# A decoder step on one core: ScalarE's DMAs issued by GpSimd, and the first head's loads of the prompt attention ahead of other work

## The chip, the core and the metric

The kernel runs on one core of a Trainium2 chip. A core has five engines with a queue of instructions each, worked in order: TensorE (PE), VectorE (DVE), ScalarE (ACT), GpSimd (POOL) and SyncE (SP, which here only issues DMAs). SP, ACT and POOL can issue DMAs; an instruction that waits for a semaphore holds all that stand behind it on its engine. PE's clock has two levels here, 1.2 and 2.4 GHz; the profile gives the granted clock as a part of full speed. The metric is the time of one execution on the device in microseconds (us), lower is better.

## The reference

One layer of a decoder, for a prompt of 1024 rows and 8 samples of 8 new tokens with a window of 2048 cached keys and values, all in float32:

```python
yp = _half_ffn(yp, ffn1_norm[l], ffn1_w1[l], ffn1_w3[l], ffn1_w2[l])
m, kp, vp, sp = _mix_prompt(_rmsnorm(yp, mix_norm[l]), ...)
yp = yp + m
yp = _half_ffn(yp, ffn2_norm[l], ffn2_w1[l], ffn2_w3[l], ffn2_w2[l])
# the same for the samples, ys, with _mix_sample over the cached window and the state
```

`_half_ffn` is x + (silu(h w1) * (h w3)) w2 / 2 on the normalised h. The mixing step projects h to queries, keys and values of 12 heads of 64 (queries and keys normalised by head) and to queries, keys, values, gates and decays of 4 heads of a gated linear attention (GLA). The 12 heads attend in three dilated branches, whose results are merged by their log-sums; the GLA runs in chunks of 16 with a state between chunks. Both go, the GLA normalised and gated with silu(rb), through `w_out`. Returned are both outputs, the windows of keys and values (for the samples: the cached rows moved on by the 8 new ones) and the GLA states.

## The kernel before

The kernel's stages follow each other on PE, in us from the span's start: the first FFN to about 822, a mixed stage to 1244, the prompt attention to 1519, the output projection to about 1612, the second FFN to 2400. A float32 operand is split into a high and a low part, and a product is made of three matmuls.

In the mixed stage `_interleave` (L1271) runs two programs side by side. `inputs` makes the projections column block by column block: for each, weights are loaded by SP (`raw`), split (`hl`), multiplied into PSUM (`psg`, L306) in three pieces of rows, and a piece is turned and stored. `beside` is first the GLA within its chunks, then the attention of the samples (`sample`), which for each of six pairs of heads loads keys `kt` (3 buffers), values `vt` (6 buffers) and biases `sbias` by SP.

The stores that ACT issues before are these. For a block of values, `turn_values` (L421) transposes a piece on PE into `psv` (L427, L429), ACT copies it to `v` (L431, L433; 4 buffers) and stores it to the output `vp` (L439), the samples' rows also to `vnew` (L434) and to the output `wv_s` (L435). `finish_gate` (L443) stores the gates to `gsc` (L446). `sample` stores new keys (`sko` to `wk`, L817) and its outputs (`soT` to `osc`, two stores, L907). POOL's queue holds, in `finish_qk` (L451), the stores of queries to `qsc` and of keys to `kT` (L473) and the copies of the samples' part (`sqk`, L475), and in `sample` the copies from it to `sqs` (L810) and `kt` (L827); `psA` (L831) is the score product of the samples with `kt`.

In the prompt attention a second `_interleave` (L1280) runs `attention` and `linear_states` side by side. `attention` loads a head's `f` (queries from `qsc`, keys from `kT`, each in two halves of 64 rows, L929) and `bias` (L937), for every second head `va` (L940); DVE makes `q` and `kk` of them (L932 to L935; for later heads POOL makes the low parts); PE makes scores `psS` (L962), DVE adds the bias and takes the maximum (`e`, L969), ACT the exponentials (L982), PE transposes (L1001) and multiplies with `va` (`psO`, L1022). `linear_states` loads `g7` from `gsc` and `asc` (L596, L598), makes `gw` and `qm` of it on DVE (L611 to L621), and clears `st` and `qm` on POOL (L585, L590).

A scheduler sets the order on each engine: it plays the program on a model of the engines, and `high_priority` moves what is written under it ahead by an offset. It also hands out the semaphores by which a DMA tells its end. DMAs of SP and of ACT take eight of them in turn (DMAHW0 to DMAHW7), those of POOL eight others (DMASW0 to DMASW7); a DMA waits until the one before it on its semaphore has landed.

Of the kernel before, what the change touches and what calls it, by code (L numbers as in the profile page):

```python
# [9 lines left out]
F32 = mybir.dt.float32  # L10
# [6 lines left out]
P = 128  # L17
# [103 lines left out]
class _Kernel:  # L121
# [299 lines left out]
    def turn_values(self, pool, ps, z, m, ci):  # L421
        nc, a = self.nc, self.a
        cols = slice(128 * m, 128 * m + 128)
        t0, nt = 3 * ci, 3 if ci < 2 else 2
        p = ps.tile([P, 512], F32, tag="b", name="psv")
# [6 lines left out]
        if ci == 2:  # L432
            nc.scalar.copy(v[:64, 2], p[:64, 256:384])  # L433
            nc.scalar.dma_start(out=self.vnew[:, cols], in_=v[:64, 2])  # L434
            nc.scalar.dma_start(  # L435
                out=a["wv_s"].rearrange("b (r c) -> b r c", c=768)[:, 2040:2048, cols], in_=v[:64, 2]
            )
            self.vdone = m + 1
        nc.scalar.dma_start(  # L439
            out=a["vp"][128 * t0 : 128 * (t0 + nt), cols].rearrange("(t p) c -> p t c", p=P), in_=v[:, :nt]  # L440
        )

    def finish_gate(self, z, m, ci):  # L443
        nc = self.nc
        nc.scalar.activation(z, z, AF.Silu)
        nc.scalar.dma_start(  # L446
            out=self.gsc[3 * ci : 3 * ci + 3, :, 5 + m].rearrange("t p r -> p t r"),
            in_=z.rearrange("p (t r) -> p t r", t=3),
        )
# [131 lines left out]
    def linear_states(self, pool, ps):  # L581

        nc, a = self.nc, self.a
        st = pool.tile([P, 9, 64], F32, tag="st", name="st", bufs=2)
        nc.gpsimd.memset(st[:, 0], 0.0)  # L585
        ms = pool.tile([P, 3, 36], F32, tag="gms", name="gms")
        qm = []
# [48 lines left out]
        for T in range(9):  # L636
# [11 lines left out]
            for j, src in enumerate((kdT, g[:, 3], g[:, 4])):  # L648
# [3 lines left out]
                out=kx,  # L652
# [125 lines left out]
    def sample(self, pool, ps, loadk):  # L778
# [18 lines left out]
        for i in range(6):  # L797
# [8 lines left out]
            for e in range(2):  # L806
# [9 lines left out]
            nc.scalar.copy(ko, p[:64, :128])  # L816
            nc.scalar.dma_start(  # L817
                out=a["wk"].rearrange("b (r c) -> b r c", c=768)[:, 2040:2048, 128 * i : 128 * i + 128], in_=ko
# [87 lines left out]
            for e in range(2):  # L906
                nc.scalar.dma_start(  # L907
                    out=self.osc[i, 64 * e : 64 * e + 64].rearrange("p (b t) -> p b t", t=8), in_=t[:, :, e]
                )
# [3 lines left out]

    def attention(self, inputs, pool, ps):
        nc = self.nc
        heads = {}

        def load(h):
# [18 lines left out]
            nc.sync.dma_start(out=b, in_=bass.AP(z.tensor, z.offset + 127, [[GW - 1, P], [1, NP]]))  # L937
            if e == 0:
                v = pool.tile([P, 8, 128], F32, tag="v", name="va", bufs=2)
                nc.sync.dma_start(  # L940
                    out=v, in_=self.a["vp"][:, 128 * i : 128 * i + 128].rearrange("(t p) c -> p t c", p=P)
                )
            else:
                v = heads[h - 1][3]
            heads[h] = (q, kh, kl, v, b)

        def scores(h, g):

            q, kh, kl, v, b = heads[h]
            out = []  # L950
# [58 lines left out]
        def weigh(h, g, es, pts):  # L1009
            i, e = h // 2, h % 2  # L1010
            r = slice(64 * e, 64 * e + 64)
            v = heads[h][3]
            if g % 2 == 0 and e == 0:
# [26 lines left out]
        self.tc.keep_in_program_order(nc.scalar.preload_act_table_set(LOG_EXP))  # L1040
        load(0)
        yield 10
# [104 lines left out]
    def run(self):  # L1147
        nc, tc, a = self.nc, self.tc, self.a
        self.gready, self.done, self.vdone = False, 0, 0
        with ExitStack() as top:  # L1150
            self.dram = top.enter_context(tc.tile_pool(name="dram", bufs=1, space=DRAM))
# [121 lines left out]
            with ExitStack() as hs:  # L1273
                hpool(hs)
                with ExitStack() as bs:
# [3 lines left out]
                    states = (4.6 * c for c in self.linear_states(gp, ps0))  # L1279
                    _interleave(tc, [(self.attention(ip, ap, ps0), 0), (states, 0)])  # L1280
                with pool("wts") as wp, pool("xp", side="right") as xp:
# [165 lines left out]
```

## Time and profile before

| | us |
|---|---|
| three executions | 2400.91, 2401.41, 2404.52 (median 2401.41) |
| the profiled execution, its time | 2401.93 |
| its span, first to last instruction | 2400.1 |
| its mean granted clock of PE | 0.989 |
| PE busy | 2341.4 |
| DVE, ACT, POOL busy | 1155.9, 656.9, 408.3 |

The profile is of one execution. PE is the engine that is busy nearly throughout, so the reader should look for the stretches where it isn't, and then for what ended last before it went on. ACT's DMA queue moves 5.11 MB in 16512 packets, SP's 316.39 MB.

### The profile page before, as it was taken

What the parts mean: (1) busy time and instruction counts of PE and PEld (TensorE: products, weight loads), DVE (VectorE), ACT (ScalarE), POOL (GpSimd) and SP (SyncE); (2) the same over time, 40 slices, a digit from 0 to 9 for tenths busy, and PEclk for the clock granted to TensorE, in tenths of its full rate; (3) what the DMA queues carried; (4) which work ended last, traced back from release to release, by engine and by line L of the source; (5) the groups of instructions that cost most, each with busy time, mean ns of one, the idle gap of its engine ahead of it and who ended that gap; (6) DMA issues with size and microseconds to landing.
All of it is one profiled execution on the core that took longest, in us unless ns stands there. A gap on an engine that the chain in (4) does not pass through costs nothing.

```text
span 2400.1 us, 38321 instructions
## 1 busy us (share of the span) xinstructions
PE 2341.4 (98%) x16073; PEld 2215.0 (92%) x16073; DVE 1155.9 (48%) x2377; ACT 656.9 (27%) x1347; POOL 408.3 (17%) x303
## 2 busy tenths in 40 slices
PE   7999999999999998999989999999999999999999
PEld 6999999999999987978767767999999999999999
DVE  8452434344342753555538887435444342434333
ACT  5111020101101522545436666334111101020110
POOL 5011020101100400011103231333101101020100
PEclk9999999999999999999999999999999999999999
DMA  7346542524250334599865442414244243111002
GB/s 258 110 162 192 191 152 97 210 97 153 86 196 23 134 131 108 179 342 341 310 184 130 111 115 74 156 36 158 88 163 153 92 154 143 45 53 45 28 17 85
DMA packets 135261, 330.25 MB, mean 138 GB/s; under 512 B 25920, under 2 KB 105264, under 8 KB 127408
## 3 DMA queue, kind: packets, MB, share of 16 engines
q1 hardware_dynamic: 116464, 316.39, 38.7%
q10 hardware_dynamic: 16512, 5.11, 0.9%
q0 software_dynamic: 2112, 6.29, 0.7%
q8 instruction: 126, 2.06, 0.3%
q14 instruction: 47, 0.39, 0.0%
HBM read 300.55 MB, written 134.56 MB: 181 GB/s over the span
## 4 chain that ended last, share of the span: by engine, by line
PE 89%; DVE 5%; DMA 3%; ACT 2%; issue 1%; SPq 1%; POOL 0%; ACTq 0%; DVEq 0%; POOLq 0%
PE ps L306 42%; PE ps L257 21%; PE psg L306 12%; PE pso L306 4%; PE psO L1022 2%; PE psS L962 2%; PE psW L880 1%; PE psT L1001 1%; DMA vt<-in_vin 1%; PE psA L831 1%; DVE hL L155 1%; DVE e L969 1%; PE pss L459 1%; DMA f<-out_kT 0%; DVE rstd L170 0%
## 5 line engine op out<-in xcount | busy, mean ns | idle before, releaser
L306 PE MATMUL ps<-hH,hl 128*128 128x362 f32 (+1 forms) x4224 | 1044.1, 328 | 8.1 <-ACT hl L130 6.8
L306 PEld LDWEIGHTS ps<-hH,hl 128*128 128x128 f32 x4224 | 746.6, 188 | 12.4 <-ACT hl L130 6.7
L306 PE MATMUL ps<-hL,hl 128*128 128x362 f32 (+1 forms) x2112 | 691.5, 328 | 2.9 <-DVE hL L155 2.9
L257 PE MATMUL ps<-g,hl 128*128 128x362 f32 (+1 forms) x3168 | 529.2, 328 | 0.0
L257 PEld LDWEIGHTS ps<-g,hl 128*128 128x128 f32 x3168 | 527.0, 188 | 0.0
L134 POOL TENSOR_TENSOR hl<-raw,hl 128x1024 fp32r<-128x1024 f32 (+1 forms) x98 | 242.8, 2498 | 1223.3 <-ACT hl L130 1223.3
L306 PEld LDWEIGHTS ps<-hL,hl 128*128 128x128 f32 x2112 | 397.5, 188 | 4.9 <-DVE hL L155 3.9
L306 PE MATMUL psg<-hH,hl 128*128 128x384 f32 (+3 forms) x1200 | 312.4, 334 | 0.0
L262 DVE SCALAR_TENSOR_TENSOR xT<-ps,xT 128x362 f32<-128x362 f32 (+1 forms) x384 | 204.6, 534 | 200.3 <-PE ps L257 191.4
L217 ACT ACTIVATE t<-t 128x364 f32<-128x364 f32 x132 | 66.9, 508 | 786.0 <-DVE t L216 785.8
L218 DVE TENSOR_TENSOR t<-ps,rstd 128x364 f32<-128x364 f32 x132 | 70.6, 535 | 417.9 <-PE ps L306 417.9
L306 PEld LDWEIGHTS psg<-hH,hl 128*128 128x128 f32 (+1 forms) x1200 | 211.3, 186 | 12.8 <-issue 8.9
L306 PE MATMUL psg<-hL,hl 128*128 128x384 f32 (+3 forms) x600 | 200.1, 334 | 0.1
L130 ACT CAST hl<-raw 128x1024 fp32r<-128x1024 f32 (+2 forms) x148 | 124.1, 886 | 187.3 <-PE ps L306 109.9
L130 ACT CAST g<-t 128x364 fp32r<-128x364 f32 x132 | 65.2, 494 | 346.8 <-DVE t L219 346.8
L134 DVE TENSOR_TENSOR g<-t,g 128x364 fp32r<-128x364 f32 x132 | 107.1, 813 | 92.8 <-ACT g L130 92.5
L216 DVE TENSOR_TENSOR t<-ps,rstd 128x364 f32<-128x364 f32 x132 | 70.5, 535 | 156.6 <-PE ps L306 155.3
L306 PEld LDWEIGHTS psg<-hL,hl 128*128 128x128 f32 (+1 forms) x600 | 111.7, 186 | 9.3 <-issue 6.7
L134 DVE TENSOR_TENSOR hl<-raw,hl 128x384 fp32r<-128x384 f32 (+3 forms) x178 | 102.9, 587 | 23.9 <-ACT hl L130 19.9
L962 PE MATMUL psS<-kk,q 128*128 128x512 f32 (+2 forms) x288 | 92.2, 411 | 19.6 <-DVE s L969 11.9
L306 PE MATMUL pso<-hH,hl 128*128 128x362 f32 (+1 forms) x384 | 93.6, 325 | 0.2 <-DVE o L1032 0.2
L982 ACT ACTIVATE e<-e,s 128x128 f32<-128x128 f32 (+3 forms) x96 | 74.9, 780 | 43.7 <-DVE s L969 43.1
(205 smaller groups left out, 2007.2 us busy)
## 6 DMA issues: line engine op xcount, KB each, us to landing
out_wk<-in_ck SPq DMA_DIRECT2D x16, 3060.0 KB
out_wv_s<-in_cv SPq DMA_DIRECT2D x16, 3060.0 KB
kt<-in_kin SPq DMA_DIRECT2D x24, 1280.0 KB
vt<-in_vin SPq DMA_DIRECT2D x60, 512.0 KB
raw<-in_w13b SPq DMA_DIRECT2D x22, 1024.0 KB
raw<-in_w13a SPq DMA_DIRECT2D x21, 1024.0 KB
raw<-in_w2a SPq DMA_DIRECT2D x48, 192.0 KB
raw<-in_w2b SPq DMA_DIRECT2D x48, 192.0 KB
```

The lines of the kernel that those rows point to most:

```text
L130: nc.scalar.copy(hi, x)
L134: e.tensor_tensor(out=lo, in0=x, in1=hi.bitcast(F32), op=ALU.subtract)
L155: nc.vector.scalar_tensor_tensor(out=self.hL[:, k, s], in0=x, scalar=g, in1=self.hH[:, k, s].bitcast(F32), op0=ALU.mult, op1=ALU.subtract)
L216: nc.vector.tensor_tensor(out=t1[:, :n], in0=p1[:, :n], in1=r, op=ALU.mult)
L217: nc.scalar.activation(t1[:, :n], t1[:, :n], AF.Silu)
L218: nc.vector.tensor_tensor(out=t3[:, :n], in0=p3[:, :n], in1=r, op=ALU.mult)
L257: self.mm(p[:, :n], lhsT=hl[:, wt, j, :], rhs=g[:, gp, :n], start=i == 0, stop=i == 3 * nf - 1)
L262: nc.vector.scalar_tensor_tensor(out=xs, in0=p[:, :n], scalar=0.5, in1=xs, op0=ALU.mult, op1=ALU.add)
L306: self.mm(p[:m, :n], lhsT=hl[:, wt, k, cs], rhs=h[:, k, h0 : h0 + n], start=i == 0, stop=i == 23)
L962: self.mm(p[:, :mm], lhsT=q[:, 128 * n : 128 * n + 128], rhs=kk[:, o : o + mm], start=x == 0, stop=x == 1,)
L982: nc.scalar.activation(e[:, :w], e[:, :w], AF.Exp, scale=-1.0, bias=s[:, j : j + 1], accum_out=s[:, 2:3])
L1022: self.mm(p[64 * n : 64 * n + 64, :128], lhsT=v[:, k, r], rhs=pts[k // 2][k, n], start=k == 0, stop=k == 2 * g + n, tile_position=(0, 64 * n),
```

## The change

All DMAs that ACT issued are issued by POOL. The load of `va` becomes a method, `load_v`: the first is written at the start of `linear_states`, the others stay in `attention`'s `load` for even heads; its buffers move from the pool `att` to `gst`. `load(0)` stands under `high_priority(offset=300)`. The two programs of the prompt attention are handed to `_interleave` in the other order. A head's raw rows come in two transfers for each operand, as before. Lines after L586 have numbers one to eight higher in the changed kernel.

```diff
@@ turn_values @@
         nc.scalar.copy(v[:, :nt].rearrange("p t c -> p (t c)"), p[:, : 128 * nt])
         if ci == 2:
             nc.scalar.copy(v[:64, 2], p[:64, 256:384])
-            nc.scalar.dma_start(out=self.vnew[:, cols], in_=v[:64, 2])
-            nc.scalar.dma_start(
+            nc.gpsimd.dma_start(out=self.vnew[:, cols], in_=v[:64, 2])
+            nc.gpsimd.dma_start(
                 out=a["wv_s"].rearrange("b (r c) -> b r c", c=768)[:, 2040:2048, cols], in_=v[:64, 2]
             )
             self.vdone = m + 1
-        nc.scalar.dma_start(
+        nc.gpsimd.dma_start(
             out=a["vp"][128 * t0 : 128 * (t0 + nt), cols].rearrange("(t p) c -> p t c", p=P), in_=v[:, :nt]
         )
@@ finish_gate @@
         nc.scalar.activation(z, z, AF.Silu)
-        nc.scalar.dma_start(
+        nc.gpsimd.dma_start(
             out=self.gsc[3 * ci : 3 * ci + 3, :, 5 + m].rearrange("t p r -> p t r"),
@@ linear_states @@
         nc.gpsimd.memset(st[:, 0], 0.0)
+        self.load_v(pool, 0)
@@ sample @@
             nc.scalar.copy(ko, p[:64, :128])
-            nc.scalar.dma_start(
+            nc.gpsimd.dma_start(
                 out=a["wk"].rearrange("b (r c) -> b r c", c=768)[:, 2040:2048, 128 * i : 128 * i + 128], in_=ko
             )
...
             for e in range(2):
-                nc.scalar.dma_start(
+                nc.gpsimd.dma_start(
                     out=self.osc[i, 64 * e : 64 * e + 64].rearrange("p (b t) -> p b t", t=8), in_=t[:, :, e]
                 )
@@ new, and attention @@
+    def load_v(self, pool, i):
+        v = pool.tile([P, 8, 128], F32, tag="v", name="va", bufs=2)
+        self.nc.sync.dma_start(
+            out=v, in_=self.a["vp"][:, 128 * i : 128 * i + 128].rearrange("(t p) c -> p t c", p=P)
+        )
+        self.values[i] = v
+
-    def attention(self, inputs, pool, ps):
+    def attention(self, inputs, pool, vpool, ps):
...
-            if e == 0:
-                v = pool.tile([P, 8, 128], F32, tag="v", name="va", bufs=2)
-                nc.sync.dma_start(
-                    out=v, in_=self.a["vp"][:, 128 * i : 128 * i + 128].rearrange("(t p) c -> p t c", p=P)
-                )
-            else:
-                v = heads[h - 1][3]
-            heads[h] = (q, kh, kl, v, b)
+            if h % 2 == 0 and h:
+                load_v(i)
+            heads[h] = (q, kh, kl, b)
...
-        load(0)
+        with self.tc.high_priority(offset=300):
+            load(0)
@@ run @@
-                    _interleave(tc, [(self.attention(ip, ap, ps0), 0), (states, 0)])
+                    _interleave(tc, [(states, 0), (self.attention(ip, ap, gp, ps0), 0)])

```

On ACT, at the fourth block of values (in the trace around 945 us), before, in the order of the queue; `Activation` and `PE` are semaphores of those engines:

```order
L431 COPY v<-psv 128x384 [waits DMAHW5_49,PE_49]
L439 DMA out_vp<-v 128x3x128 [waits DMAHW1_49,Activation_49]
L431 COPY v<-psv 128x256 [waits DMAHW6_49,PE_49]
L433 COPY v<-psv 64x128
L439 DMA out_vp<-v 128x2x128 [waits DMAHW0_49,Activation_49]
L434 DMA vnew<-v 64x128 [waits DMAHW2_49,Activation_49]
L435 DMA out_wv_s<-v 8x8x128 [waits DMAHW4_49]
L431 COPY v<-psv 128x384 [waits PE_49]
L439 DMA out_vp<-v 128x3x128 [waits DMAHW6_49,Activation_49]
```

and now:

```order
L431 COPY v<-psv 128x384 [waits DMASW2_49,PE_49,Activation_49]
L431 COPY v<-psv 128x256 [waits DMASW3_49,PE_49,Activation_49]
L433 COPY v<-psv 64x128
L431 COPY v<-psv 128x384 [waits DMASW5_49,DMASW4_49,DMASW6_49,PE_49,Activation_49]
L130 CAST hl<-raw 128x512 [waits DMAHW0_49,DVE_49,PE_49]
L130 CAST hl<-raw 128x512
L431 COPY v<-psv 128x384 [waits DMASW7_49,PE_49,Activation_49]
L431 COPY v<-psv 128x256 [waits DMASW0_49,PE_49,Activation_49]
L433 COPY v<-psv 64x128
```

The stores stood between the copies; now the copies of three blocks stand with the weight splits alone.

On SP, at the start of the prompt attention, before (`g_` are the tiles `g7`):

```order
L794 DMA vt<-in_vin 128x1024 [waits PE_49]
L940 DMA va<-out_vp 128x8x128 [waits DMAHW5_49,DVE_49,Pool_49]
L940 DMA va<-out_vp 128x8x128 [waits DMAHW6_49,Activation_49]
L929 DMA f<-qsc 64x1024 [waits DMASW2_49,DMAHW0_49,DMASW1_49,DMASW0_49]
L929 DMA f<-qsc 64x1024 [waits DMAHW1_49]
L929 DMA f<-out_kT 64x1024 [waits DMASW5_49,DMAHW2_49,DMASW4_49,DMASW3_49]
L929 DMA f<-out_kT 64x1024 [waits DMAHW3_49]
L937 DMA bias<-Z 128x1024 [waits DMAHW4_49,PE_49]
L596 DMA g_11144<-gsc 128x640 [waits DMAHW5_49]
L598 DMA g_11144<-asc 128x4x128 [waits DMAHW6_49]
```

and now:

```order
L795 DMA vt<-in_vin 128x1024 [waits DMAHW7_49,DMAHW0_49,PE_49]
L937 DMA f<-qsc 64x1024 [waits DMASW2_49,DMASW3_49,DMASW1_49,DVE_49]
L937 DMA f<-qsc 64x1024 [waits DMAHW1_49]
L937 DMA f<-out_kT 64x1024 [waits DMASW6_49,DMAHW2_49,DMASW5_49,DMASW4_49]
L937 DMA f<-out_kT 64x1024 [waits DMAHW3_49]
L945 DMA bias<-Z 128x1024 [waits DMAHW4_49,PE_49]
L917 DMA va<-out_vp 128x8x128 [waits DMAHW5_49]
L597 DMA g_11129<-gsc 128x640 [waits DMAHW6_49,Pool_49]
L599 DMA g_11129<-asc 128x4x128 [waits DMAHW7_49]
```

The four loads of `f` moved ahead of both loads of `va`, and one of those went behind the second head's loads.

On POOL, at the second pair of heads of the samples' attention, before:

```order
L810 COPY sqs<-sqk 64x4x8 x3
L473 DMA out_kT<-z 128x384 [waits DMASW7_49,DVE_49]
L473 DMA out_kT<-z 128x384 [waits DMASW0_49,DVE_49]
L473 DMA out_kT<-z 128x256 [waits DMASW1_49,DVE_49]
L475 COPY sqk<-z 128x64 [waits Pool_49]
L827 COPY kt<-sqk 128x8x8 [waits DMAHW1_49,DMAHW4_49,PE_49,Pool_49]
```

and now:

```order
L811 COPY sqs<-sqk 64x4x8 x3
L473 DMA out_kT<-z 128x384 [waits DMASW4_49,DVE_49]
L908 DMA osc<-soT 512x1x8 [waits DMASW5_49,Activation_49]
L908 DMA osc<-soT 512x1x8 [waits DMASW6_49]
L473 DMA out_kT<-z 128x384 [waits DMASW7_49,DVE_49]
L473 DMA out_kT<-z 128x256 [waits DMASW0_49,DVE_49]
L475 COPY sqk<-z 128x64 [waits Pool_49]
L828 COPY kt<-sqk 128x8x8 [waits DMAHW6_49,DMAHW3_49,DMAHW7_49,PE_49,Pool_49]
```

The two stores of `osc` came between the first and the second store of keys, ahead of the copies to `sqk` and `kt`.

## Rows read from the trace of the kernel before

**Rows 1.** The page, busy time of the engines in us, with the share of the span and the number of instructions.

```profile
PE 2341.4 (98%) x16073; PEld 2215.0 (92%) x16073; DVE 1155.9 (48%) x2377; ACT 656.9 (27%) x1347; POOL 408.3 (17%) x303
```

**Rows 2.** Busy time by stretch. The stretch in us from the span's start, its length, then busy us of PE, of its weight loads, DVE, ACT and POOL (with the number of instructions), the granted clock of PE as a part of full speed, the busy share of the 16 DMA engines, GB/s.

```profile
937.00:960.00 23.00, 14.23 (x84) 13.84 (x83) 1.05 (x3) 0.85 (x4) 0.00 (x0) 0.82 0.76 171
...
1040.00:1080.00 40.00, 40.00 (x328) 32.19 (x328) 21.94 (x48) 19.46 (x42) 4.67 (x13) 1.00 1.02 360
...
1244.00:1300.00 56.00, 43.76 (x457) 33.47 (x458) 40.85 (x112) 32.03 (x86) 17.98 (x13) 0.85 0.62 161
1300.00:1400.00 100.00, 93.70 (x1177) 72.67 (x1176) 86.33 (x266) 67.25 (x183) 26.47 (x20) 0.98 0.43 117
1400.00:1519.00 119.00, 110.67 (x1273) 87.31 (x1271) 89.33 (x276) 82.08 (x212) 27.97 (x19) 0.96 0.30 86
```

**Rows 3.** Waits of PE in 903 to 965 us: what waited, for what, us in total, times, longest.

```profile
PE psv L427 <- ACT v L431: 8.8, 1, 8.8
```

**Rows 4.** Timeline of ACT around 945 us: start, us, engine (ACTq is its queue issuing a DMA), line, operation, out<-in; in brackets the idle time before and what ended it.

```profile
937.04 0.26 ACT L433 COPY v<-psv 64x128 f32<-64x128 f32 x1
954.63 0.38 ACTq L439 DMA_DIRECT2D out_vp<-v  x1
...
956.82 0.64 ACTq L435 DMA_DIRECT2D out_wv_s<-v  x1
957.51 0.48 ACT L431 COPY v<-psv 128x384 f32<-128x384 f32 x1 [20.20 <-DMA vt<-in_vin]
```

**Rows 5.** Timeline of SP's DMA queue in the same stretch; the second number is the time from the wait's end to the issue of the row's last DMA.

```profile
941.22 3.91 SPq L799 DMA_DIRECT2D sbias<-sB  x1
...
946.20 3.73 SPq L794 DMA_DIRECT2D vt<-in_vin  x5
```

**Rows 6.** The chain that ended last, its pieces in 930 to 965 us in order of time: start, us, what.

```profile
936.74 4.19 PE psg L306 x24
...
946.20 10.60 DMA vt<-in_vin
```

**Rows 7.** Timeline of PE in the same stretch (x2: two matmuls; a row's second number is from the first one's start to the last one's end).

```profile
947.20 0.34 PE L306 MATMUL psg<-hL,hl 128*128 128x384 f32 x1
...
948.24 0.34 PE L306 MATMUL psg<-hL,hl 128*128 128x384 f32 x1
...
958.04 0.69 PE L427 MATMUL psv<-ident,zv 128*128 128x128 f32 x2 [8.77 <-ACT v L431]
...
959.06 0.52 PE L306 MATMUL psg<-hL,hl 128*128 128x384 f32 x1
...
961.94 0.37 PE L306 MATMUL psg<-hL,hl 128*128 128x384 f32 x1
```

**Rows 8.** DMA issues in 1000 to 1130 us: out<-in, queue, number, KB each, median us from issue to landing.

```profile
qsc<-z POOLq DMA_DIRECT2D x6, 192.0 KB, 6.3
```

**Rows 9.** Waits of PE in 960 to 1240 us.

```profile
PE pss L459 <- ACT sqhl L130: 1.2, 1, 1.2
PE psW L880 <- DMA vt<-in_vin: 1.1, 3, 0.5
```

**Rows 10.** Timeline of POOL at the second head of the sample attention.

```profile
1084.73 0.54 POOL L473 DMA_DIRECT2D out_kT<-z  x1 [6.74 <-DVE z L468]
...
1085.62 0.24 POOL L827 COPY kt<-sqk 128x64 f32<-128x64 f32 x1
```

**Rows 11.** Timeline of ACT there.

```profile
1082.18 0.25 ACT L905 COPY soT<-psY 64x128 f32<-64x128 f32 x1
...
1083.28 1.72 ACTq L907 DMA_DIRECT2D osc<-soT  x2
```

**Rows 12.** Timeline of PE there.

```profile
1088.75 1.31 PE L831 MATMUL psA<-kt,sqs 128*32 128x328 f32 x16
```

**Rows 13.** Timeline of SP's DMA queue where the prompt attention begins.

```profile
1237.09 1.01 SPq L940 DMA_DIRECT2D va<-out_vp  x2
1238.26 6.00 SPq L929 DMA_DIRECT2D f<-qsc  x2
1245.28 1.11 SPq L929 DMA_DIRECT2D f<-out_kT  x2
...
1247.54 0.50 SPq L598 DMA_DIRECT2D g<-asc  x1
```

**Rows 14.** Timeline of DVE there.

```profile
1244.28 0.21 DVE L404 TENSOR_TENSOR zr<-psg,rstd 128x64 f32<-128x64 f32 x1
1247.33 1.03 DVE L932 CAST q<-f 128x1024 fp32r<-128x1024 f32 x1 [2.83 <-DMA f<-qsc]
1248.39 1.22 DVE L933 TENSOR_TENSOR q<-f,q 64x1024 fp32r<-64x1024 f32 x1
1249.98 0.69 DVE L934 CAST kk<-f 128x1024 fp32r<-128x1024 f32 x1 [0.36 <-DMA f<-out_kT]
...
1258.88 0.29 DVE L611 TENSOR_TENSOR gw<-g 128x128 f32<-128x128 f32 x1 [3.43 <-DMA g<-gsc]
```

**Rows 15.** Timeline of PE there.

```profile
1250.82 0.77 PE L962 MATMUL psS<-kk,q 128*128 128x256 f32 x2 [6.91 <-DVE kk L934]
```

**Rows 16.** Waits of PE in 1243 to 1519 us.

```profile
PE psS L962 <- DVE s L969: 11.9, 11, 2.0
...
PE psO L1022 <- ACT rb L1018: 4.7, 4, 2.2
```

More of the change, by code (lines that the diff above doesn't have):

```diff
@@ L937, in load, with load_v @@
             nc.sync.dma_start(out=b, in_=bass.AP(z.tensor, z.offset + 127, [[GW - 1, P], [1, NP]]))
-            if e == 0:
-                v = pool.tile([P, 8, 128], F32, tag="v", name="va", bufs=2)
-                nc.sync.dma_start(
-                    out=v, in_=self.a["vp"][:, 128 * i : 128 * i + 128].rearrange("(t p) c -> p t c", p=P)
-                )
-            else:
-                v = heads[h - 1][3]
-            heads[h] = (q, kh, kl, v, b)
+            if h % 2 == 0 and h:
+                load_v(i)
+            heads[h] = (q, kh, kl, b)
+        def load_v(i):
+            self.load_v(vpool, i)
         def scores(h, g):
-            q, kh, kl, v, b = heads[h]
+            q, kh, kl, b = heads[h]
             out = []
@@ L1011, in weigh @@
             r = slice(64 * e, 64 * e + 64)
-            v = heads[h][3]
+            v = self.values[i]
             if g % 2 == 0 and e == 0:
@@ L1149, in run @@
         self.gready, self.done, self.vdone = False, 0, 0
+        self.values = {}
         with ExitStack() as top:
```

## The prediction

> **What bounds the kernel now.** I read the page first, then the busy time by stage, then the waits of the engine that is busy. TensorE (PE) is busy for 98% of the span [rows 1], so only stretches where it idles or runs at the lower clock can give time back. The diff touches nothing before the values of the projections in the mixed stage and nothing after the attention, 1519 us, but one load's place, so I looked at what lies between. By stage PE is full but for two places [rows 2]: 937 to 960 us, with 14.23 us of work in 23, and the prompt attention from 1244 us, with 43.76 in 56 at a clock of 0.85 at its start and 8.3 us idle in its last 119.
>
> The first place has one cause. PE waits once, 8.8 us, in the transposes of the values (L427), for ScalarE's (ACT's) copy at L431 that empties the PSUM tile [rows 3]. ACT had nothing to compute: it copied a piece of v at 937.04 and then stood until 954.63, when it issued the store of that piece (L439); two more stores follow (L434, L435), and only at 957.51 came the copy that PE wanted [rows 4]. In the order of the kernel before, that L439 store waits for DMAHW0, and so does SP's load of sbias. SP issued sbias at 941.22, after 3.91 us, and five 512 KB loads of vt from 946.20 behind it [rows 5]; the chain of waits has the transfers that fill these microseconds as one piece of 10.60 us from 946.20 [rows 6]. So a 128 KB store waited for the landing of another queue's 644 KB load, in an in-order engine, with PE's PSUM behind it.
>
> **The change part by part.** *Stores from ACT to GpSimd (POOL).* In the new order ACT has no DMA: the copies at L431 follow each other and wait for PE and for stores four pieces back. The stall goes. PE lost 8.77 us of idle time before the matmul at 958.04. Then it ran at the lower clock: from 959.06 to 961.94 are nine matmuls, 0.32 us each, where the six from 947.20 to 948.24 took 0.173 each [rows 7]: 9 x 0.147 = 1.3 us, and some 0.2 us for the transposes ahead of them. Term one: 8.8 + 1.5 = **10.3 us**. What would be late next is the buffer of v: four pieces deep, a piece for each 4.19 us of the projection's matmuls [rows 6], so a store has some 17 us to land. The nearest rows, POOL's own stores of q and k, land in 6.3 us [rows 8]; in 946 to 957 us the transfers are crowded, and a store could take as long there as the vt loads, 10.6 us, still under 17. I take the whole 10.3; between it and nothing lies the second rival.
>
> Does the gain reach the end? From 960 to 1240 us PE waits 1.2 us and 1.1 us in its two largest groups [rows 9]; it is the bound there, its loads are asked for as it frees buffers (kt three deep, vt six), and so the whole stage should begin earlier and end earlier. But the transfers stand at 1.02 of their capacity in 1040 to 1080 [rows 2], which is the ground of a rival.
>
> *The price on POOL.* 54 DMAs move. POOL issues one of its stores in 0.54 us [rows 10], ACT two osc stores in 1.72 us [rows 11]. At 0.54 that is 29 us more work for an engine that is busy for 4.67 of 40 us in 1040 to 1080 [rows 2]: nothing. But each store stands in order. Before psA's last part of a head, POOL must copy the new keys into kt (L827); the new order puts the two osc stores, and the wait for soT, ahead of the second and third out_kT stores, the sqk copy and that kt copy. For the second head: soT is copied at 1082.18 to 1082.43 [rows 11], psA runs at 1088.75 [rows 12], and out_kT twice, sqk and kt take 0.54 x 2 + 0.24 x 2 = 1.56 us [rows 10]. That leaves 4.76 us for two osc stores: free up to 2.4 us each. At 0.54 to 0.86 us (POOL's own price, ACT's) nothing is lost; osc has 512 pieces of 32 B, unlike any store POOL has now, so the upper end is open. I take nothing, and the rest is the slower rival.
>
> The Trainium skill, "DMA: Bandwidth & Descriptors", section "SWDGE vs HWDGE vs iDMA", speaks against the move: the descriptors of a DMA from GpSimd are computed by a program on its cores, those of SP's and ACT's by logic, with a faster setup. By the page's first-byte figures, about 1 against 0.6 us, each store would land 0.4 us later (an estimate from that page), and with 17 us of room the sum would be the same.
>
> *The first head's loads.* Before, SP issues two va loads at 1237.09, then f<-qsc at 1238.26 for 6.00 us: the second half is held by a DMAHW lane that an ACT store holds; then f<-out_kT at 1245.28 and g<-asc at 1247.54 [rows 13]. DVE ends the projection's last piece at 1244.28 + 0.21 and then waits 2.83 us for q, 0.36 for k and 3.43 for the second g load [rows 14]; PE's first score waits 6.91 us [rows 15]. After, the four f loads come straight behind the vt loads of 1225, ahead of va, on lanes of SP's alone; they should be there before 1244.5. DVE's q cast and low part (1.03 + 1.22 us) and kk cast (0.69) still stand behind the last zr, so the first score comes at 1244.5 + 1.03 + 1.22 + 0.69 = about 1247.5 instead of 1250.82: 3.3 us. The g loads move from behind two va loads to behind one, and the second head of g (3.43 us of wait) now stands behind four more of the score pieces on DVE, so it holds none of these. If all three waits of DVE go, it is 2.83 + 0.36 + 3.43 = 6.6 us. Against it: POOL's memsets of st and qm now stand behind its own last gsc stores and their landing (6 us, by rows 8), and one DVE row of qm stands ahead of the fourth score piece. Between 3.3 and 6.6 I take **5 us**.
>
> *Swapped order of the two programs.* It alters when linear states and scores come among each other through 1519 us. PE idles 8.3 us in 1400 to 1519 [rows 2]; its largest wait there and before is 11.9 us in eleven pieces for DVE's score step (L969), next 4.7 us for ACT's rb [rows 16]. Neither is aimed at. A new order may win or lose some of it; I set 0, with 5 us to each side, about a third of the 16.6 us of these two. The load of va from the other pool and the third wout load's new place cost nothing: psO needs va only after scores, exponentials and transposes, and wout's third unit is used last.
>
> **Sum.** The profiled execution took 2401.93 us, 1.8 over its span, 0.5 over the median: 2401.9 - 10.3 - 5 = 2386.6, and by the median 2386.
>
> **The rivals.** *Only the first gain stays* (chance 0.22). The new order of attention loses what its start wins, 5 us on DVE: 2401.4 - 10.3 - 0 = 2391. For it: DVE's score step is already what PE waits for most [rows 16], and an earlier start of attention meets the same amount of DVE work. Against it: the start's waits are for loads, not for work.
>
> *The transfers take it back* (0.12). If the store's wait was only the sign of full transfers (1.02 of capacity in 1040 to 1080), then PE runs ahead 10 us and waits 10 us for kt and vt. Price: all of term one; the start of attention may keep its 0 to 5 us, so 2397 to 2402. For it: rows 2. Against it: PE waits only 1.1 us for vt in three pieces now [rows 9], and since the loads are released by PE's own progress they come earlier with it. The Trainium skill, the same page, section "Issuing engines are not separate DMA queues", says that the choice of the issuing engine saves only the time to issue, mostly small beside the transfer; by it the time would be near 2401. Rows 4 speak against it: 17 us went in waiting to issue, not in issuing.
>
> *POOL's queue becomes the wait* (0.12, slower). If an osc store of 512 small pieces costs POOL 5 us rather than 0.54, the two hold the kt copy by 2 x 5 - 4.8 = 5 us for a head, psA with it, for five heads and at the last one the gsc stores: 25 us or more, 2401.4 - 15 + 25 = 2411. It decides from 2 x 4 - 4.8 = 3.2 us a head, 16 us in all, so from 4 us for one store. For it: POOL's price for small pieces isn't in the trace. Against it: two stores of 192 and 128 KB cost it the same 0.54 us.
>
> *A larger gain* (0.08): the start wins 6.6 us and the new order 5 more: 2401.4 - 10.3 - 11.6 = 2380.
>
> **How the numbers follow.** The forecast, 2386 with 5 to each side, has 0.46; the rivals 0.22 at 2391, 0.12 at 2397 to 2402, 0.12 at 2404 to 2412, 0.08 at 2380. About 0.2%, 5 us, is what a measurement can tell from no change. Faster: 0.46 + 0.22 + 0.08 = 0.76; the same 0.12; slower 0.12. The range leaves out the slower rival and the last 2 us of the third (0.16 in all), and reaches 2 us below the lowest case, since the new order's 5 us are no hard bound: 2378 to 2400.
>
> **What would show it.** Right: PE's wait for L431 near 945 to 957 gone and the clock there at its higher level; first score some 13 us earlier (10 + 3); no wait of DVE for f or for the first g. Wrong: PE waiting for kt, vt or psA in 960 to 1230 (second or third rival), POOL's osc stores over 2.4 us each, or PE idle after 1300 us above the 14.6 us of now [rows 2]. Wrong from the start would be a v copy still standing for a store's landing.

## The result, and the profile after

The changed kernel takes 2384.27 us, median of four runs (2382.72 to 2384.68); the kernel before, in the runs on the same chip and those above, 2401.16. The ratio is 0.9929, 95% interval 0.9912 to 0.9946: faster by about 17 us. The profiled execution took 2382.72 us, its span 2381.0, at a mean granted clock of 0.995.

The page of the changed kernel, busy time of the engines [against rows 1], and POOL's DMA queue (packets, MB, share of the 16 engines):

```profile
PE 2333.7 (98%) x16073; PEld 2208.8 (93%) x16073; DVE 1152.6 (48%) x2377; ACT 655.8 (28%) x1347; POOL 446.0 (19%) x357
...
q0 software_dynamic: 4512, 11.41, 1.3%
```

Busy time by stretch, columns as in rows 2:

```profile
937.00:960.00 23.00, 23.00 (x147) 22.88 (x146) 5.24 (x9) 4.53 (x10) 5.37 (x8) 1.00 0.80 200
...
1030.00:1070.00 40.00, 40.00 (x327) 31.51 (x326) 21.79 (x45) 21.16 (x46) 7.28 (x17) 1.00 0.93 334
1234.00:1290.00 56.00, 48.41 (x570) 36.79 (x570) 49.55 (x142) 36.56 (x103) 20.34 (x17) 0.94 0.64 179
1290.00:1390.00 100.00, 92.02 (x1185) 72.47 (x1184) 85.78 (x255) 66.15 (x181) 30.17 (x22) 0.98 0.41 115
1390.00:1500.00 110.00, 100.34 (x1157) 79.41 (x1155) 82.13 (x259) 77.45 (x198) 24.65 (x16) 0.98 0.29 82
```

The first place is gone: 937 to 960 us is full (23.00 of 23, against 14.23), at the higher level of the clock throughout. Transfers are no fuller in the stage behind it (0.93 against 1.02). At the start of the attention PE works 48.41 of 56 us at a clock of 0.94 (43.76 at 0.85). Later it idles more than before, not less: 8.0 and 9.7 us in the two long stretches, against 6.3 and 8.3. So the attention's gain lies at its beginning. The prediction had more than 14.6 us of idle there as a sign of being wrong; 17.6 came, and the attention is shorter all the same, because what PE gained is not idle time alone (the part on the prediction shows it).

ACT around the place of the stall [against rows 4], then PE there [rows 7]:

```profile
935.14 0.26 ACT L433 COPY v<-psv 64x128 f32<-64x128 f32 x1
939.42 0.48 ACT L431 COPY v<-psv 128x384 f32<-128x384 f32 x1 [4.02 <-issue]
...
947.78 0.37 ACT L431 COPY v<-psv 128x256 f32<-128x256 f32 x1 [3.35 <-issue]
```

```profile
947.21 0.38 PE L427 MATMUL psv<-ident,zv 128*128 128x128 f32 x2
...
951.71 0.27 PE L427 MATMUL psv<-ident,zv 128*128 128x128 f32 x1
```

ACT copies a piece of v every 4 us or so and never waits for a store. PE comes to the transposes at 947.21, where it was at 958.04 before, and into the next ones at 951.71.

The stores now stand on POOL (the second number is the issue):

```profile
944.72 0.75 POOL L439 DMA_DIRECT2D out_vp<-v  x1 [3.75 <-ACT v L431]
948.44 0.72 POOL L439 DMA_DIRECT2D out_vp<-v  x1 [2.96 <-ACT v L433]
949.15 0.56 POOL L434 DMA_DIRECT2D vnew<-v  x1
949.71 0.62 POOL L435 DMA_DIRECT2D out_wv_s<-v  x1
```

A store of v takes POOL 0.72 to 0.78 us. Those issued in 931 to 963 us land 4.9 to 10.0 us after the issue began; the slowest is the one of 944.72, landed at 954.74. So the crowded transfers do hold the stores, by nearly the 10.6 us that the prediction allowed for, and the 17 us of room were enough. At the second head of the samples, POOL [rows 10] and PE's psA [rows 12]:

```profile
1066.78 1.36 POOL L908 DMA_DIRECT2D osc<-soT  x2 [4.00 <-ACT soT L906]
...
1072.88 0.55 POOL L473 DMA_DIRECT2D out_kT<-z  x1 [4.18 <-DVE z L468]
1073.48 0.24 POOL L475 COPY sqk<-z 128x64 f32<-128x64 f32 x1
1073.78 0.24 POOL L828 COPY kt<-sqk 128x64 f32<-128x64 f32 x1
```

```profile
1077.79 1.31 PE L832 MATMUL psA<-kt,sqs 128*32 128x328 f32 x16
```

Two osc stores take 1.36 us, 0.68 each. The kt copy ends at 1074.02, 3.8 us before psA needs it.

What PE waits for vt in the stage (one group of its waits), and the same seen at its weight loads (busy and mean ns, then idle time before them and what ended it), before from 964.56 and now from 951.71 to the end of the projections:

```profile
PE psW L881 <- DMA vt<-in_vin: 1.6, 2, 0.9
```

```profile
L880 PEld LDWEIGHTS psW<-vt,spt 128*32 128x32 f32 x480 | 14.8, 109 | 12.5 <-issue 6.6 <-DMA vt<-in_vin 0.8
L881 PEld LDWEIGHTS psW<-vt,spt 128*32 128x32 f32 x480 | 14.9, 109 | 12.5 <-issue 4.4 <-DMA vt<-in_vin 3.1 <-DMA raw<-in_wqk 0.2
```

The start of the attention: SP's queue [rows 13], DVE [rows 14], PE [rows 15], and the largest waits of PE in the attention [rows 16]:

```profile
1217.36 1.16 SPq L937 DMA_DIRECT2D f<-qsc  x2
1218.69 1.83 SPq L937 DMA_DIRECT2D f<-out_kT  x2
...
1231.19 0.43 SPq L917 DMA_DIRECT2D va<-out_vp  x1
```

```profile
1234.65 0.21 DVE L404 TENSOR_TENSOR zr<-psg,rstd 128x64 f32<-128x64 f32 x1
1234.78 0.68 DVE L940 CAST q<-f 128x1024 fp32r<-128x1024 f32 x1
1235.50 1.22 DVE L941 TENSOR_TENSOR q<-f,q 64x1024 fp32r<-64x1024 f32 x1
1236.75 0.69 DVE L942 CAST kk<-f 128x1024 fp32r<-128x1024 f32 x1
...
1239.38 0.29 DVE L975 CUSTOM_DVE_ANT_0 e<-psS,bias 128x128 f32<-128x128 f32 x1 [0.68 <-PE psS L968]
```

```profile
1237.50 0.80 PE L968 MATMUL psS<-kk,q 128*128 128x256 f32 x2 [3.23 <-DVE kk L942]
```

```profile
PE psS L968 <- DVE s L975: 8.2, 14, 1.3
PE psO L1028 <- ACT rb L1024: 4.8, 3, 3.2
```

f is asked for at 1217 to 1220, 14 to 17 us before DVE's last zr, so the three steps that PE waits for follow it without a gap, and the first score comes 3.5 us behind the last projection matmul (1233.96), against 7.2. The first score step of DVE (L975) stands ahead of gw now, and nothing holds it for a load.

### The profile page after: what moved, and what is told of

Same layout as the page of the kernel before. It is cut to its first block, busy times and chain, and to the rows that moved or that the text cites. A ratio compares the mean times of both kernels' runs of the same rounds, so it can differ in the third digit from the quotient of the medians.

```text
span 2381.0 us, 38372 instructions
## 1 busy us (share of the span) xinstructions
PE 2333.7 (98%) x16073; PEld 2208.8 (93%) x16073; DVE 1152.6 (48%) x2377; ACT 655.8 (28%) x1347; POOL 446.0 (19%) x357
## 3 DMA queue, kind: packets, MB, share of 16 engines
q0 software_dynamic: 4512, 11.41, 1.3%
## 4 chain that ended last, share of the span: by engine, by line
PE 90%; DVE 5%; DMA 2%; ACT 2%; issue 1%; POOL 0%; SPq 0%; DVEq 0%; ACTq 0%; POOLq 0%
PE ps L306 43%; PE ps L257 21%; PE psg L306 12%; PE pso L306 4%; PE psO L1028 2%; PE psS L968 2%; PE psA L832 1%; PE psT L1007 1%; DMA vt<-in_vin 1%; PE psW L881 1%; DVE hL L155 1%; DVE rstd L170 1%; DVE e L975 1%; PE pss L459 1%; DMA g<-gsc 0%
```

## The experiments

Each kernel ran in three to five rounds beside the kernel before (medians of it 2399.9 to 2400.2 us). The table has the median, and from each one's profiled execution the start of the last matmul of the projections, of the first score and of the first matmul of the output projection, in us; "start" is from the first of these to the second, "attention" from the first to the third.

| kernel | median | projections' last | first score | output projection | start | attention |
|---|---|---|---|---|---|---|
| before | 2401.2 | 1243.6 | 1250.8 | 1518.3 | 7.2 | 274.7 |
| changed | 2384.3 | 1234.0 | 1237.5 | 1498.8 | 3.5 | 264.8 |
| e1, DMAs only | 2392.9 | 1234.1 | 1240.0 | 1509.7 | 5.9 | 275.6 |
| e2, attention only | 2399.0 | 1241.0 | 1245.1 | 1514.8 | 4.0 | 273.7 |
| e3, values' stores only | 2396.2 | 1236.2 | 1246.0 | 1515.4 | 9.7 | 279.1 |
| e4, changed without the swap | 2384.1 | 1235.0 | 1238.5 | 1499.7 | 3.5 | 264.7 |
| e5, changed without priority | 2388.4 | 1235.1 | 1242.6 | 1506.3 | 7.5 | 271.2 |
| e6, e2 with gsc on POOL | 2394.7 | 1243.9 | 1247.5 | 1513.5 | 3.6 | 269.6 |
| e7, changed with gsc on ACT | 2390.1 | 1234.0 | 1237.5 | 1503.1 | 3.5 | 269.1 |
| e8, e1 with priority | 2389.4 | 1233.6 | 1239.1 | 1503.4 | 5.5 | 269.8 |
| e9, sbias on POOL | 2402.0 | 1245.0 | 1252.0 | 1518.2 | 7.0 | 273.2 |
| e10, values' stores on SP | 2392.1 | 1234.7 | 1242.1 | 1507.4 | 7.3 | 272.6 |
| e11, first key cast on ACT | 2390.3 | 1236.4 | 1239.3 | 1506.3 | 2.9 | 269.9 |

Two scatters are to be kept in mind. In some profiles the clock is at 0.83 to 0.91 for 10 to 20 us after 850 us, ahead of everything that the edits touch (before, e3, e6, e10), in the others it is at 1.00. The copy of v at 937.04 in rows 4 stands at 936.6 to 937.8 us in these four and at 935.0 to 935.8 in the other nine, so some 2 us of the three times are this. And the attention's length in one profile can be 5.8 us off with nothing changed: e1 and e8 turned out to work in one and the same order (below, at e8), and have 275.6 and 269.8. The medians are the firmer numbers; of e1 and e8 they lie 3.5 us apart.

**e1: all 54 DMAs on POOL, nothing else.**

```diff
-            nc.scalar.dma_start(
+            nc.gpsimd.dma_start(
```

> The kernel before with all of ACT's DMAs issued by POOL, and nothing else of the change. Theory (two separate gains: the stall of ACT's stores, about 10 us up to the end of the projections, and the start and order of the attention, about 10 us after it): the wait of PE for the v copy is gone, the last projection matmul ends about 9 to 10 us earlier, the attention keeps its length of about 274 us; 2391 us (2388 to 2395). Rival A (the attention's gain too comes from the DMAs, because f's loads no longer share semaphores with ACT's stores): 2384 to 2387. Rival B (only the attention's part gains for good, transfers take the rest back): 2397 or more.

2392.89 us (ratio 0.9965, 0.9952 to 0.9977), 7.3 us under the kernel before. PE's wait for the v copy is gone, the projections end where they do in the changed kernel, and the attention isn't shorter. The theory's number holds, the gain a little under the 9 to 10 us expected.

**e2: the attention's part only, the DMAs on ACT.**

```diff
 # the changed kernel, with
-nc.gpsimd.dma_start(   # in turn_values, finish_gate, sample
+nc.scalar.dma_start(
```

> The changed kernel with all 54 DMAs back on ACT. Theory: PE's 8.8 us wait for the v copy is back, the last projection matmul ends near 1243 us, the attention is shorter by 7 to 10 us; 2392 us (2390 to 2396). Rival A (the attention's gain needs the DMAs off ACT): attention shorter by 3 us or less, 2397 to 2401.

2398.95 us (0.9996, 0.9987 to 1.0005): no gain that can be told from nothing, rival A. The first score is early (4.0 us), but the attention keeps its length. Waits of SP's queue at its start, then of PE, then one row of ACT's timeline:

```profile
SPq L599 <- DMA gsc<-zr: 5.1, 1, 5.1
```

```profile
PE psO L1028 <- ACT rb L1024: 9.6, 5, 4.8
PE psv L427 <- ACT v L431: 9.2, 1, 9.2
```

```profile
1257.96 0.31 ACT L616 ACTIVATE gw<-g 128x128 f32<-128x128 f32 x1 [4.74 <-DMA g<-gsc]
```

SP stood 5.1 us at the load of g from asc, until ACT's last gsc store had landed: in the order both stand on DMAHW5. The loads of the second g stood behind it, ACT waited 4.74 us for that, rb behind gw, and PE 9.6 us in all for rb. So the theory of two separate gains fell. The new theory: the attention's gain needs the stores of the mixed stage's end off the semaphores that SP uses.

**e3: the stores of the values only.**

```diff
 # in turn_values only
-            nc.scalar.dma_start(
+            nc.gpsimd.dma_start(
```

> The kernel before with only the stores of turn_values (vp, vnew, wv_s: 30 of the 54 DMAs) issued by POOL. Theory: the whole gain before the attention is theirs, since the one long wait is behind such a store: 2391 us, within 3 us of the run with all DMAs moved. Rival C (the later stores on ACT, osc, out_wk and gsc, held ACT too): 4 us or more slower than the run with all DMAs moved.

2396.16 us (0.9984, 0.9975 to 0.9994), 3.3 us above e1, between the two expectations. PE waits for no v copy, so these 30 stores are the whole of the first stall. Some of its later first column is the clock at 0.91 in 850 to 870. Its profiled execution lies 3.2 us above the median. The rest shows behind the projections: the start takes 9.7 us, and SP waited there for a store that stayed on ACT:

```profile
SPq L929 <- DMA gsc<-zr: 5.6, 1, 5.6
```

**e5: the changed kernel without the priority.**

```diff
-        with self.tc.high_priority(offset=300):
-            load(0)
+        load(0)
```

> The changed kernel without high_priority at load(0); va and both g7 loads then stand ahead of f in SP's order. Theory (the priority buys the start: first score 3.5 us after the last projection matmul instead of 7.2): first score 5 to 7 us after the last projection matmul, total 2387 to 2390. Rival D (the gain after the start is the order's luck): the start is as said, but the rest of the attention moves by more than 4 us either way, so a total under 2385 or over 2392.

2388.35 us (0.9948, 0.9936 to 0.9961): 4.1 us above the changed kernel, in the range. The start is 7.5 us, a little over the 5 to 7 expected, and of the 6.4 us by which the attention is longer, 4.0 are this start. All five of its executions (2387.24 to 2390.30) are above all eight of the changed kernel and e4 (2381.86 to 2386.64).

**e6 and e7: the six gsc stores alone.** In e6 they join the attention's part on POOL, in e7 they go back to ACT from the changed kernel.

```diff
 # e6, on e2, in finish_gate; e7 is the same line the other way, on the changed kernel
-        nc.scalar.dma_start(
+        nc.gpsimd.dma_start(
```

> The attention's part with ACT's DMAs kept on ACT, except the six gsc stores of finish_gate, which POOL issues. Theory (in the run of the attention's part alone, SP's load of g from asc waited 5.1 us for the semaphore of ACT's last gsc store, and g, ACT's gw, rb and PE's psO stood behind it): that wait is gone, so are the 5.2 us of DVE and the 4.8 us of PE for rb, the attention takes 265 to 268 us instead of 273.8; PE's 9 us wait for the v copy stays; 2391 to 2394 us. Rival (the attention's gain needs ACT free of all DMAs, or POOL's queue): 2396 or more.

> The changed kernel with only the six gsc stores back on ACT. Theory: the opposite of the run before: SP's load of g from asc waits some 5 us for a gsc store's semaphore, the attention takes 271 us or more, 2389 to 2393 us; no wait of PE for the v copy. Rival (six stores among 54 don't matter): 2383 to 2386.

e6 takes 2394.66 us (0.9977, 0.9969 to 0.9986), 4.3 us under e2; e7 2390.10 (0.9955, 0.9943 to 0.9968), 5.8 above the changed kernel. Both ways the six stores carry some 5 us, as the new theory has it. Its details missed: e6 is just over the 2391 to 2394 expected and its attention is 269.6 us instead of 265 to 268; that of e7 is 269.1 instead of 271 or more. SP's queue, first of e6, then of e7:

```profile
SPq L597 <- DMA osc<-soT: 5.0, 1, 5.0
```

```profile
SPq L597 <- DMA gsc<-zr: 5.4, 1, 5.4
```

With gsc gone from the shared semaphores, the next holder was an osc store of ACT, 5.0 us at the load of g from gsc, the one ahead of the load that stood in e2; e7 stood there too. So it is no store in particular, but whichever of ACT's last stores comes before SP's load on its semaphore.

**e8: all DMAs on POOL and the priority, va still loaded in attention.**

```diff
 # on e1
-        load(0)
+        with self.tc.high_priority(offset=300):
+            load(0)
```

> All DMAs on POOL and high_priority at load(0), but va loaded in attention as before and the programs in the old order. In its order SP still has both va loads ahead of f, and DVE both gw steps ahead of the first score step. Theory (the priority works only with the va load out of load): as without priority, 2390 to 2394 us, first score 5 to 6 us after the last projection matmul. Rival (the priority alone is worth what its removal cost, 4 us): 2387 to 2389.

2389.38 us (0.9957, 0.9943 to 0.9970), 3.5 us under e1, a shade under the theory's 2390 to 2394 and at the rival's upper end. But e8 is e1 over again. In the two traces, by operation, tile and shape, DVE, ACT, POOL and SP work in the same order from the first instruction to the last, with both loads of va ahead of f, and PE too but for twelve places in the mixed stage where matmuls next to each other swap. So with va loaded in attention the priority moved nothing, as the theory has it, and the rival falls, although its number came out. The waits of DVE for the first q, in e1 and in e8, then the attention of each (columns as in rows 2, from the last projection matmul on):

```profile
DVE q L932 <- DMA f<-qsc: 2.0, 1, 2.0
```

```profile
DVE q L932 <- DMA f<-qsc: 1.8, 1, 1.8
```

```profile
1234.40:1509.80 275.40, 248.83 (x2903) 194.54 (x2902) 215.69 (x651) 179.08 (x478) 72.42 (x53) 0.93 0.40 113
```

```profile
1233.90:1503.50 269.60, 241.57 (x2902) 188.00 (x2903) 214.95 (x651) 179.11 (x478) 72.39 (x53) 0.97 0.42 115
```

The start is the same within 0.4 us, and PE idles no less in e8 (28.0 us against 26.6). It is busy 7.3 us less with the same matmuls, because the granted clock was 0.97 and not 0.93. The five executions of e1 go from 2389.15 to 2395.10 us and the five of e8 from 2387.38 to 2395.54; all ten together have a median of 2390.8, 9.3 under the 2400.1 of the kernel before. What is left to the changed kernel, 6.5 us, is the moved load of va with the priority. In the changed kernel DVE waits for neither f nor g up to the first four score steps.

**e9: the loads of sbias on POOL, nothing else.**

```diff
 # on the kernel before, in sample
-            nc.sync.dma_start(
+            nc.gpsimd.dma_start(
                 out=bias, in_=self.sB[16 * i : 16 * i + 16]...
```

> The kernel before with the loads of sbias issued by POOL, and nothing else. ACT's order stays; the semaphore of the store that stalled (L439, DMAHW0) is now held by the 2 KB load of m, and the one of the next store (L434, DMAHW2) by a 512 KB load of vt. Theory (the stall is the wait for the semaphore's holder): the L439 store goes out within 8 us of the copy instead of 17, and ACT now stands at L434 until vt has landed; PE's wait for the v copy is 2 to 7 us instead of 8.8. Rival (transfers are full and any store waits there): ACT stands at L439 as before.

2402.00 us (1.0009, 1.0000 to 1.0018). ACT's timeline, and the row of SP's queue with the 2 KB load that now holds the semaphore of the first stalled store:

```profile
935.64 0.26 ACT L433 COPY v<-psv 64x128 f32<-64x128 f32 x1
949.61 0.38 ACTq L439 DMA_DIRECT2D out_vp<-v  x1
951.47 0.48 ACTq L434 DMA_DIRECT2D vnew<-v  x1
955.62 0.64 ACTq L435 DMA_DIRECT2D out_wv_s<-v  x1
956.31 0.48 ACT L431 COPY v<-psv 128x384 f32<-128x384 f32 x1 [20.41 <-DMA out_vp<-v]
```

```profile
942.76 3.89 SPq L781 DMA_DIRECT2D m<-in_m  x1
```

The L439 store went out at 949.61, 14 us after the copy instead of 17 (8 were expected), once the small load had come (SP had issued it by 942.76 + 3.89 = 946.65). Then ACT stood at L434 and at L435, and the copy that PE wants came at 956.31. That the holder decides which store stands is borne out; that the stall would shrink is not: PE waited 9.0 us. The stall is spread over three stores, each with another holder, and taking one holder away gives nothing.

**e10: the values' stores on SP.**

```diff
 # on the kernel before, in turn_values
-            nc.scalar.dma_start(
+            nc.sync.dma_start(
```

> The kernel before with the stores of turn_values issued by SP in place of ACT, nothing on POOL. They share the eight DMAHW semaphores as before, but what waits for one is now SP. Theory (what cost PE its 8.8 us was that ACT, which empties PSUM, stood in order behind its stores): PE's wait for the v copy is 0 to 3 us, the last projection matmul ends 4 to 9 us earlier; 2391 to 2396 us. Rival (the stores must have semaphores of their own, or be off the full queue): the wait stays over 5 us through v's four buffers, 2397 us or more.

2392.11 us (0.9966, 0.9952 to 0.9979), as e1 with nothing moved to POOL. The stores still share the semaphores, and still wait; ACT's copies then wait for v's buffers:

```profile
945.41 0.47 ACT L431 COPY v<-psv 128x384 f32<-128x384 f32 x1
953.25 0.37 ACT L431 COPY v<-psv 128x256 f32<-128x256 f32 x1 [7.36 <-DMA out_vp<-v]
```

A copy waited 7.36 us for a store to land, but PE waited for no copy: the four buffers cover it. So it wasn't POOL's queue that helped, but that ACT, which empties PSUM, no longer stands in order behind stores.

**e11: the first head's key cast on ACT.**

```diff
 # on the changed kernel, in attention's load
-            nc.vector.tensor_copy(kh, f[1])
+            if h:
+                nc.vector.tensor_copy(kh, f[1])
+            else:
+                nc.scalar.copy(kh, f[1])
```

> The changed kernel with the first head's key cast (L942) on ACT, beside DVE's cast and low part of q. Theory (the first score now waits for three DVE steps, 0.68 + 1.22 + 0.69 us, behind the last zr): first score 0.5 to 0.7 us earlier, total 2383 to 2385 us, not to be told from the changed kernel. Rival (ACT's cast stands behind its table loads, and the first exponential behind it): first score later, 2386 us or more.

2390.30 us (0.9951, 0.9936 to 0.9965): 6 us slower than the changed kernel, a miss. The first score did come 0.6 us sooner after the last projection matmul (two rows of PE's timeline), and nothing behind ACT was late there:

```profile
1236.41 0.31 PE L306 MATMUL psg<-hH,hl 128*128 128x320 f32 x1
1239.32 0.54 PE L971 MATMUL psS<-kk,q 128*128 128x256 f32 x2 [2.60 <-DVE q L941]
```

But its projections end 2.4 us later, though up to there every engine works in the changed kernel's order (PE but for six places of neighbouring matmuls), and the attention behind the first score takes 267.0 us where the changed kernel's takes 261.3. In the attention some twenty places of DVE's order changed. PE does not idle more there (24.1 us against 25.0). It is busy 6.0 us more with the same matmuls, at a clock of 0.95 instead of 0.97 (the row of the changed kernel stands in the next part):

```profile
1236.70:1506.40 269.70, 245.62 (x2903) 193.33 (x2902) 216.81 (x650) 180.52 (x479) 72.94 (x53) 0.95 0.40 113
```

So the loss is time at the lower level. Whether the new order brings it about or this set of executions had it by chance is open: the five go from 2385.30 us (mean clock 0.995) to 2392.54 (0.993).

**e4: the changed kernel without the swap.**

```diff
-                    _interleave(tc, [(states, 0), (self.attention(ip, ap, gp, ps0), 0)])
+                    _interleave(tc, [(self.attention(ip, ap, gp, ps0), 0), (states, 0)])
```

> The changed kernel with the two programs of the attention in the old order of the list. The instructions' order differs in 14 lines on PE and 12 on DVE from the changed kernel's. Theory (the swap does nothing by itself): 2383 to 2386 us. Rival (it carries part of the attention's gain): 2388 us or more.

2384.10 us (0.9931, 0.9918 to 0.9945): the swap does nothing. In the two traces, by operation, tile and shape, DVE, ACT, POOL and SP again work in the same order, and PE but for a few neighbouring matmuls of the mixed stage. No version beat the changed kernel.

## Why the prediction was right, and where its terms were off

**The total** was 2386, measured 2384.3; the likeliest case was the one that came. Its signs came too: PE's wait is gone at the higher level, the first score is 13.3 us earlier, DVE waits for neither f nor the first g. By the medians the first term is some 9.3 us (e1 and e8 together) of the 10.3 forecast, the rest 6.5 of 5. The terms' insides were less good than their sum.

**Term one, 10.3 us, was mis-sized at its end, not at its place.** At its place it is 10.8 us: PE reaches the transposes after the stall 12.7 us sooner (964.40 before, 951.71 now), and 1.9 of these it had already ahead of the stall, where the profile of the kernel before has its low clock.

```profile
964.40 0.49 PE L427 MATMUL psv<-ident,zv 128*128 128x128 f32 x3
```

At the end of the projections 9.6 us are left, or 7.7 without that 1.9. So the step "does the gain reach the end" failed by 3 us. From the transposes to the last projection matmul the same work takes 282.3 us instead of 279.2. It is no scatter of one profile: in three of the four that have the stall this stretch takes 277.5 to 279.2 us and in the fourth, e9, 281.6; in the nine without it 281.6 to 284.2. The second rival named the transfers for it. PE's matmuls wait 1.6 us for vt there, against 1.1. Its weight loads have 3.1 us put down to vt, against 0.8, but their idle time at that line is 12.5 us in both, so this isn't a loss. What is shown of the transfers is half a microsecond; the rest of the 3 us is not settled.

**The cause of the stall** was put down rightly to a store waiting for a semaphore that SP's load held (e9), and the cost to ACT standing in order (e10). The prediction named one holder, the sbias load; there are several, one behind the other. By the Trainium skill, "DMA: Bandwidth & Descriptors", section "Issuing engines are not separate DMA queues", the gain should have been the issue time only; e10 and e1 speak against that for this kernel: they gain 8.0 and 7.3 us, where a store took 0.38 to 0.64 us to issue [rows 4], since what went was waiting to issue.

**POOL's price** was rightly set at nothing: 0.68 us for an osc store, under the 2.4 us that were free, and kt ready 3.8 us ahead of psA. The slower rival's point, 4 us a store, is far off. POOL has 37.7 us more work, not 29, and it costs nothing. Stores of v land within 10.0 us of the 17 allowed.

**The first head's loads, 5 us.** The start came as worked out: the first score 3.5 us behind the last projection matmul, 3.7 us better, where 3.3 were forecast, by the same three DVE steps (the first took 0.68 us instead of 1.03). By the medians the whole term is 6.5 us, at its upper bound of 6.6; in the two profiles the attention is 9.9 us shorter. Two things were missing in it. First, it was put beside the DMAs as if it came alone; alone it is worth 1.3 us, not to be told from nothing (e2), because ACT's last gsc and osc stores hold the semaphores of SP's next loads (e6, e7). Second, it counted waits alone. The prediction named the clock of 0.85 at the attention's start and gave it no price. The attention before and now, from the end of the last projection matmul:

```profile
1243.90:1518.40 274.50, 247.64 (x2903) 193.25 (x2902) 216.04 (x651) 180.86 (x479) 71.82 (x52) 0.94 0.41 113
```

```profile
1234.30:1498.90 264.60, 239.63 (x2902) 188.09 (x2903) 216.43 (x651) 178.75 (x478) 74.02 (x53) 0.97 0.41 115
```

PE idles 26.9 us before and 25.0 now, so only 1.9 of the 9.9 us are waits. The other 8.0 are the same matmuls in less busy time, at a clock of 0.97 instead of 0.94. By the clock's records in the traces PE stood at 1.2 GHz for 30.7 us of the attention before and for 13.7 now, 27.0 and 11.1 of them busy; half of the difference of these is 8.0 us. Before, the clock first fell at 1248.70, in the 6.91 us that PE idled ahead of the first score [rows 15]; now at 1236.50, in the 3.23 us there, and it came back sooner. In all thirteen profiles the busy time, with that at the lower level counted half, is 233 to 237 us, so what tells their attentions apart is this level and, in e3 (33.9 us against 24 to 28), idle time.

Most of the gain lies in the first heads: from the key cast of the first head to that of the fourth it is 38.8 us instead of 44.4, from there to the twelfth 178.1 and 178.8. The steps, by medians: the priority is worth 4.1 us once va is out of attention (e5) and nothing with it there (e8); va's move without the priority 2.4 (e5 against e1 and e8), less than the scatter; the swap nothing (e4), as forecast.

**That a new order may win or lose 5 us** was forecast as the swap's risk. That was not put to the test: the swap left the order as it was (e4).

**The first rival**, the start's gain lost on DVE, fell: PE waits 8.2 us for DVE's score step now, against 11.9. That the attention gains nothing is what came in e2, but by waits for loads, not on DVE.

## What to carry to other kernels

An engine that empties PSUM should not issue stores whose semaphore another queue's large loads can hold: a wait of a DMA holds all that is behind it, and it shows as idle time of the engine with a DMA as its releaser and nothing to compute. Moving the stores to any queue that can afford to stand (here SP as well as POOL) gave the gain. Two edits at one place should be priced together: the early loads paid only once the stores that held their semaphores were gone. A wait of the engine that bounds a kernel costs more than its idle time when the clock falls in it: 8.0 of the 9.9 us in the attention were that, and a list of waits doesn't show them. And before a small difference is put down to an edit, the order that was really run should be compared: e8 had the order of e1, and their medians of five executions lay 3.5 us apart.

## What was not expected of the hardware

The moved 5.11 MB went as 16512 packets on ACT's queue and as 2400 on POOL's (4512 less the 2112 of before). A store of osc, 512 rows of 32 B in the program, costs POOL 0.68 us to issue, a store of keys of 128 rows 0.54: four times the rows cost a quarter more. A 2 KB load in the crowded stretch of e9 held its semaphore for about 3 us.
